# Residual turnings: one tile and one trip through DRAM for both token halves, reads issued by Pool's queue, users six steps on

## The chip, the cores and the metric

The kernel runs on one core of one Trainium2 chip. The engines that matter here are TensorE (PE in the rows; PEld is its weight load), VectorE (DVE), ScalarE (ACT), GpSimd (Pool, POOL) and SyncE (SP), each with an instruction queue of its own that runs in order. SP does no arithmetic: it issues DMA transfers, which 16 DMA engines carry out. The metric is the device time of one launch in microseconds, as a median of runs, lower being better.

## The reference

One decoder block in float32: 256 tokens, model width 2048, SwiGLU width 5632. Every matrix product keeps float32 accuracy.

```python
h = h + 0.5 * swiglu(rms_norm(h, ffn1_norm), ffn1_w_gate, ffn1_w_up, ffn1_w_down)
n = rms_norm(h, mix_norm)
rq, rk, rv, rg, sq, sk, sv = split(n @ w_in)
ret = groupnorm(retention(rope(rq), rope(rk), rv)) * silu(rg)       # 8 heads of 128, chunks of 128
swa = sliding_window_attention(rope(sq), rope(sk), sv, sinks)       # 16 query heads of 64, window 128
h = h + concat(ret, swa) @ w_out
h = h + cross_attention(rms_norm(h, xa_norm), rms_norm(mem, mem_norm))   # 4 heads of 512, 256 memory tokens
h = h + 0.5 * swiglu(rms_norm(h, ffn2_norm), ffn2_w_gate, ffn2_w_up, ffn2_w_down)
out = rms_norm(h, final_norm)
```

## The kernel before

**Products.** A float32 product is made of three: both operands are split into a rounded part and the rest (`halves`, lines 73 to 76: ScalarE writes the rounded copy, VectorE subtracts), and `three` (line 468) multiplies high by high, high by low and low by high. The weights come from DRAM in pieces of 1 MB, two steps to a piece, into three buffers `wf`, and are split into `wh` and `wl`, four buffers each.

**Steps.** `run_stream` (line 232) walks 772 steps. A step is 12 matmuls of 128 x 512 on one split weight piece: two inner blocks, two token halves of 128, three products. A clock counts the steps. In step *at* the work that has come due runs first (`run_due`), then weights are split up to three steps ahead (`prepare`, LOOKAHEAD) and fetched up to seven steps ahead (`fetch`, AHEAD), then come the matmuls. `later(d, f)` puts a piece of work d steps on. A `Unit` is one block of 512 output columns with its accumulator in PSUM; when its last step is done it calls `done`. The order of the SP queue is pinned to that of the program, so SP issues weight loads and everything else strictly one after another.

**Turnings.** The residual stream `hT` and the operands of the next product are wanted with channels on the partitions, while a unit's result has tokens there. `cross` (line 434) turns 256 tokens by 512 columns without TensorE: VectorE transposes 32 x 32 blocks of each token half (line 444), one step later SP writes each half, 256 KB, to a `box` in DRAM (line 449), two steps later SP reads each box back in four pieces of 64 KB, in which the 32-row blocks change places (line 456), and `delay` steps later (TURN, 5) the user `then` runs. There are 54 turnings: 22 in the two SwiGLUs (`up_done`, users `halves_of`), 16 at the ends of `to_h` (first down projection twice, `w_out`, `xa_wo`; the user adds to `hT`), 4 for retention's queries and keys (`rqk_done`, user `finish`), 8 for cross attention's keys and queries (`put_done`), and 4 that turn the finished residual back for the last stage (`turn_h`, user a ScalarE copy at line 948). Those four are put 6, 10, 14 and 18 steps after the second norm's last block (line 1005), at the start of the second SwiGLU.

**Work tiles.** Tiles `t2k` of 128 x 512 have ten buffers; a turning takes two, and two more for what it reads unless its caller hands in a place. `spread` (line 412) makes a row of the mix norm's factors with two transposes on TensorE; `ret_scores` (line 740) makes the retention scores two and three steps after `finish`, and `rv_done` uses them four and five steps after its own unit.

Of the kernel before, what the change touches and what calls it, by code (L numbers as in the profile page):

```python
# [17 lines left out]
P = 128  # L18
# [15 lines left out]
FIRST = 16  # L34
TURN = 5
SWA_EVERY = 5
# [3 lines left out]
def decoder_block(ctx: ExitStack, tc: tile.TileContext, a: dict, out: bass.AP):  # L40
# [20 lines left out]
    def t2k(dt=F32):  # L61
        return work.tile([P, 512], dt, tag="t2k", name=nm("t2k"), bufs=10)

# [26 lines left out]
    nc.vector.tensor_copy(identr, ident)  # L90
    ones = const.tile([P, P], F32, tag="ones", name="ones")
    nc.vector.memset(ones, 1.0)
# [265 lines left out]
    class Norm:  # L358
# [39 lines left out]
        def finish(self):  # L398

            x = self.sums  # L400
            nc.vector.tensor_tensor(x[:, :S], x[:, :S], x[:, S:], ALU.add)
            tp = tmp_ps()
            for t in range(2):
                nc.tensor.matmul(tp[:, t : t + 1], x[:, t * P : (t + 1) * P], ones[:, :1], start=True, stop=True)
            ms = sm(2, "ms")
            nc.vector.tensor_scalar(ms, tp[:, :2], 1.0 / D, EPS, ALU.mult, ALU.add)
            nc.gpsimd.tensor_tensor(self.rs, ms, mhalf[:, :2], ALU.pow)
            self.ready = True
            if self.spreads:
                later(3, self.spread)  # L410

        def spread(self):

            tp = tmp_ps()
            for t in range(2):
                rep = t2k()[:, :P]
                nc.vector.tensor_scalar(rep, ones, self.rs[:, t : t + 1], None, ALU.mult)
                nc.tensor.transpose(tp[:, t * P : (t + 1) * P], rep, ident)
            self.rows = work.tile([P, S], F32, tag="rows", name=nm("rows"), bufs=1)
            copy(self.rows, tp[:, :S])  # L420

# [11 lines left out]

    def cross(src, then, room=None, delay=TURN):

        room = [None, None] if room is None else room
        boxes = []  # L440
        out = []
        sq = [t2k() for _ in src]
        for x, v in zip(sq, src):
            nc.vector.transpose(x.rearrange("p (g q j) -> p q g j", g=4, q=4), squares_of(v))  # L444

        def write():
            for x in sq:
                boxes.append(dram.tile([P, 512], F32, tag="box", name=nm("box")))
                nc.sync.dma_start(boxes[-1], x)

        def read():
            for box, dst in zip(boxes, room):
                dst = t2k() if dst is None else dst
                far = box.rearrange("(i r) (g n) -> g r i n", i=4, g=4)
                for g in range(4):
                    nc.sync.dma_start(dst[32 * g : 32 * g + 32, :].rearrange("p (i n) -> p i n", i=4), far[g])
                out.append(dst.rearrange("p (i q j) -> p q i j", i=4, q=4))
        later(1, write)
        later(2, read)
        later(delay, lambda: then(out))  # L460

# [13 lines left out]
    def to_h(w, lhs, factor, blocks, norm=None, then=None):  # L475

        def done(acc, b):
# [11 lines left out]
            else:  # L489
                s = [t2k() for _ in range(2)]  # L490
                for t in range(2):
                    copy(s[t], acc[:, t, :], scale=factor)
                cross(s, add, s)
        for b in range(4):
            Unit(w, b, 512, lhs, lambda acc, b=b: done(acc, b), blocks, pair=True)

    def ffn(norm, w_gate, w_up, down):
# [12 lines left out]
        def up_done(b):  # L510
            def done(acc):
# [4 lines left out]
                def made(out):  # L516
                    acts[b] = halves_of(out, blk())
                cross(s, made, s)
            return done
# [193 lines left out]
    def rqk_done(g, which):  # L713
        def done(acc):
            def finish(out):
# [18 lines left out]
                if which == 1:  # L734
                    for i in range(4):
                        later(2 + i // 2, lambda i=i: ret_scores(g, i, qk))
            cross([acc[:, t, :] for t in range(2)], finish)
# [107 lines left out]
    def put_done(norm, dst, i, then=None):  # L845

        def done(acc):
            s = [scaled(acc, t, 512, norm) for t in range(2)]

            def made(out):  # L850
                dst[i] = halves_of(out, blk())
                if then is not None:
                    later(1, then)
            cross(s, made, s)
        return done
# [146 lines left out]
    def begin_ffn2(b):  # L1002
        if b == 3:
            for b in range(4):
                later(6 + 4 * b, lambda b=b: turn_h(b))

# [85 lines left out]
```

## Time and profile before

| | before |
|---|---|
| median of 3 runs | 2200.8 us |
| lowest and highest run | 2198.17 and 2201.48 us |
| profiled execution, own time | 2198.31 us |
| its span | 2196.5 us |
| TensorE busy | 2175.0 us, 99% |
| VectorE, ScalarE, GpSimd busy | 1291.7, 1027.5 and 10.4 us |
| mean granted TensorE clock | 0.998 |
| DMA | 472.04 MB, 215 GB/s |

The page gives busy time by engine, the span in 40 slices, the chain of work that ended last and the costliest lines. A busy share averages over stages, so the places where TensorE waits were looked for in the waits and in stretches of the timeline. Window rows give, for each stretch, its length and then busy time and instructions of PE, PEld, DVE, ACT and POOL, the granted clock (1.00 is 2.4 GHz, and half of that is the other level), the DMA engines' busy share and GB/s.

### The profile page before, as it was taken

Reading aid. Unit: us, or ns where it says so; the run is one execution under the profiler, and the core shown is the slowest. Engines: PE = TensorE matmul, PEld = TensorE weight load, DVE = VectorE, ACT = ScalarE, POOL = GpSimd, SP = SyncE. Lnnn points to the kernel's source line nnn. Section 1 sums busy time; section 2 is a strip of 40 time slices with the busy share of each in tenths; the row PEclk is TensorE's granted clock in tenths of the full one; section 3 lists DMA queues with packets and bytes.
Section 4 is the critical chain, followed back from the end, with each engine's and each line's share of the span. In section 5 each row is a group of like instructions: output and inputs, shape, how many; then the busy total and the mean of one; then the engine's idle time right before and its main releaser. Section 6 shows DMA issues by size and latency. Waiting matters only on the chain.

```text
span 2196.5 us, 25627 instructions
## 1 busy us (share of the span) xinstructions
PE 2175.0 (99%) x9844; PEld 1804.2 (82%) x9844; DVE 1291.7 (59%) x1536; ACT 1027.5 (47%) x1258; POOL 10.4 (0%) x17
## 2 busy tenths in 40 slices
PE   9999999999999999999999999999899999999998
PEld 7888888888888888888888888887788888888886
DVE  6555555455556778886775555575555544555554
ACT  6444444444445554544564544454444433444443
POOL 0000000000000000000000000000000000000000
PEclk9999999999999999999999999999999999999999
DMA  7766677667667555556867654676766655666663
GB/s 269 233 217 211 216 228 232 215 214 234 206 222 262 201 185 191 174 191 207 270 232 245 215 174 171 210 250 214 246 214 215 226 196 195 215 207 220 216 215 144
DMA packets 187451, 472.04 MB, mean 215 GB/s; under 512 B 15552, under 2 KB 71616, under 8 KB 187200
## 3 DMA queue, kind: packets, MB, share of 16 engines
q1 hardware_dynamic: 187040, 470.22, 63.7%
q8 instruction: 77, 1.26, 0.2%
q14 instruction: 46, 0.38, 0.1%
q10 hardware_dynamic: 288, 0.18, 0.0%
HBM read 439.93 MB, written 30.41 MB: 214 GB/s over the span
## 4 chain that ended last, share of the span: by engine, by line
PE 95%; DVE 2%; DMA 1%; issue 1%; ACT 0%; SPq 0%; ACTq 0%; POOLq 0%; POOL 0%; DVEq 0%
PE acc L471 31%; PE acc L472 31%; PE acc L470 31%; DMA wf<-in_ffn_w_up 1%; DVE wl L76 1%; PE tmp L471 0%; PE tmp L472 0%; PE tmp L470 0%; ACT wh L71 0%; PE tmp L646 0%; DMA t2k<-box 0%; PE tmp L620 0%; DVE t2k L730 0%; DVE t2k L444 0%; PE tmp L742 0%
## 5 line engine op out<-in xcount | busy, mean ns | idle before, releaser
L76 DVE TENSOR_TENSOR wl<-wf,wh 128x1024 fp32r<-128x1024 f32 (+1 forms) x776 | 942.8, 1217 | 810.0 <-ACT wh L71 803.0
L71 ACT ACTIVATE wh<-wf 128x1024 fp32r<-128x1024 f32 (+1 forms) x776 | 817.4, 1056 | 1014.1 <-PE acc L472 955.9
L470 PE MATMUL acc<-wh,blk 128*128 128x512 f32 (+1 forms) x3104 | 1208.1, 389 | 4.4 <-ACT wh L71 3.2
L471 PE MATMUL acc<-wl,blk 128*128 128x512 f32 (+1 forms) x3104 | 1206.4, 389 | 4.7 <-DVE wl L76 4.6
L472 PE MATMUL acc<-wh,blk 128*128 128x512 f32 (+1 forms) x3104 | 1205.9, 388 | 0.0
L471 PEld LDWEIGHTS acc<-wl,blk 128*128 128x128 f32 x3104 | 583.3, 188 | 125.4 <-DVE wl L76 6.8
L470 PEld LDWEIGHTS acc<-wh,blk 128*128 128x128 f32 x3104 | 583.3, 188 | 124.4 <-ACT wh L71 3.6
L472 PEld LDWEIGHTS acc<-wh,blk 128*128 128x128 f32 x3104 | 583.1, 188 | 120.7 <-DVE blk L356 0.4
L444 DVE STREAM_TRANSPOSE t2k<-t2k 128x512 f32<-128x512 f32 x76 | 49.4, 687 | 16.8 <-ACT t2k L71 16.8
L71 ACT ACTIVATE blk<-t2k 128x512 fp32r<-128x512 f32 (+2 forms) x74 | 44.8, 608 | 9.2 <-DMA t2k<-box 7.3
L76 DVE TENSOR_TENSOR blk<-t2k,blk 128x512 fp32r<-128x512 f32 (+1 forms) x66 | 44.2, 672 | 0.0
L507 ACT ACTIVATE t2k<-acc,n 128x512 f32<-128x512 f32 x44 | 27.9, 686 | 31.6 <-PE acc L472 31.5
L514 DVE SCALAR_TENSOR_TENSOR t2k<-acc,n,t2k 128x512 f32<-128x512 f32 x44 | 31.0, 746 | 15.6 <-PE acc L472 15.6
L71 ACT ACTIVATE blk<-tmp 128x512 fp32r<-128x512 f32 (+2 forms) x53 | 23.9, 459 | 27.5 <-DVE blk L76 19.0
L71 ACT ACTIVATE blk<-h,gains 128x256 fp32r<-128x256 f32 x64 | 27.3, 496 | 5.7 <-DVE h L481 5.7
L356 DVE SCALAR_TENSOR_TENSOR blk<-h,gains,blk 128x256 fp32r<-128x256 f32 x64 | 26.9, 479 | 1.7 <-ACT blk L71 1.7
L393 DVE TENSOR_TENSOR t2k<-t2k,t2k 128x512 f32<-128x512 f32 x35 | 24.0, 685 | 2.3 <-ACT t2k L389 1.0
L76 DVE TENSOR_TENSOR blk<-tmp,blk 64x256 fp32r<-64x256 f32 (+2 forms) x45 | 22.2, 494 | 4.8 <-ACT blk L71 4.5
L471 PE MATMUL tmp<-blk,blk 128*128 128x256 f32 (+1 forms) x80 | 22.6, 282 | 0.6 <-DVE blk L76 0.6
L472 PE MATMUL tmp<-blk,blk 128*128 128x256 f32 (+1 forms) x80 | 22.5, 282 | 0.0
L470 PE MATMUL tmp<-blk,blk 128*128 128x256 f32 (+1 forms) x80 | 22.5, 281 | 0.0
L481 DVE TENSOR_TENSOR h<-h,t2k 128x512 f32<-128x512 f32 x32 | 21.0, 684 | 0.0
(122 smaller groups left out, 433.0 us busy)
## 6 DMA issues: line engine op xcount, KB each, us to landing
wf<-in_ffn_w_down SPq DMA_DIRECT2D x88, 1024.0 KB, 4.9
wf<-in_ffn_w_gate SPq DMA_DIRECT2D x87, 1024.0 KB, 5.1
wf<-in_ffn_w_up SPq DMA_DIRECT2D x87, 1024.0 KB, 5.2
box<-t2k SPq DMA_DIRECT2D x108, 256.0 KB, 2.1
t2k<-box SPq DMA_DIRECT2D x432, 64.0 KB, 4.7
wf<-in_w_in_rqk SPq DMA_DIRECT2D x16, 1024.0 KB, 5.1
wf<-in_w_in_rvg SPq DMA_DIRECT2D x16, 1024.0 KB, 5.0
wf<-in_w_out SPq DMA_DIRECT2D x16, 1024.0 KB, 5.1
```

What stands on the lines that cost most here:

```text
L71: return nc.scalar.activation(dst, src, AF.Copy, **kw)
L76: nc.vector.tensor_tensor(lo, src, hi, ALU.subtract)
L356: nc.vector.scalar_tensor_tensor(x[:, k, 1, :], v[:, k, :], g, x[:, k, 0, :], ALU.mult, ALU.subtract)
L393: nc.vector.tensor_tensor(self.sums, self.sums, y, ALU.add)
L444: nc.vector.transpose(x.rearrange("p (g q j) -> p q g j", g=4, q=4), squares_of(v))
L470: nc.tensor.matmul(o, ah, bh, start=start, stop=False)
L471: nc.tensor.matmul(o, ah, bl, start=False, stop=False)
L472: nc.tensor.matmul(o, al, bh, start=False, stop=stop)
L481: nc.vector.tensor_tensor(v, v, out[t], ALU.add)
L507: nc.scalar.activation(gated[b][t], acc[:, t, :], AF.Silu, scale=norm.scale(t))
L514: nc.vector.scalar_tensor_tensor(s[t], acc[:, t, :], norm.scale(t), s[t], ALU.mult, ALU.mult)
```

## The change

`cross` takes one new tile `t4k` of 128 x 2 x 512 (two buffers) for both token halves. The two VectorE transposes write into it; SP writes it to one box of 512 KB with one DMA; four DMAs of 128 KB, now issued from Pool's queue, read it back into the same tile; the user runs six steps on instead of five. No caller hands in a place any more. `t2k` goes from ten buffers to seven, and `ones` shrinks to one column. `spread` leaves its two transposes to a piece of work two steps later. Retention's scores come four and five steps after `finish` instead of two and three. The four turnings of the residual at the second SwiGLU stand 19, 35, 51 and 67 steps on instead of 6, 10, 14 and 18.

```diff
@@ -32,7 +32,7 @@
 TAIL = 4
 WARM = 9
 FIRST = 16
-TURN = 5
+TURN = 6
 SWA_EVERY = 5
 
 
@@ -59,7 +59,7 @@
         return work.tile([P, 4, 2, S], dt, tag="blk", name=nm("blk"), bufs=13)
 
     def t2k(dt=F32):
-        return work.tile([P, 512], dt, tag="t2k", name=nm("t2k"), bufs=10)
+        return work.tile([P, 512], dt, tag="t2k", name=nm("t2k"), bufs=7)
 
     def tmp_ps(dt=F32):
         return ps_tmp.tile([P, 512], dt, tag="tmp", name=nm("tmp"))
@@ -88,7 +88,7 @@
     make_identity(nc, ident)
     nc.vector.memset(mhalf, -0.5)
     nc.vector.tensor_copy(identr, ident)
-    ones = const.tile([P, P], F32, tag="ones", name="ones")
+    ones = const.tile([P, 1], F32, tag="ones", name="ones")
     nc.vector.memset(ones, 1.0)
     warm = tmp_ps()
     for _ in range(WARM):
@@ -401,7 +401,7 @@
             nc.vector.tensor_tensor(x[:, :S], x[:, :S], x[:, S:], ALU.add)
             tp = tmp_ps()
             for t in range(2):
-                nc.tensor.matmul(tp[:, t : t + 1], x[:, t * P : (t + 1) * P], ones[:, :1], start=True, stop=True)
+                nc.tensor.matmul(tp[:, t : t + 1], x[:, t * P : (t + 1) * P], ones, start=True, stop=True)
             ms = sm(2, "ms")
             nc.vector.tensor_scalar(ms, tp[:, :2], 1.0 / D, EPS, ALU.mult, ALU.add)
             nc.gpsimd.tensor_tensor(self.rs, ms, mhalf[:, :2], ALU.pow)
@@ -411,13 +411,18 @@
 
         def spread(self):
 
-            tp = tmp_ps()
+            rep = t2k()[:, :S]
             for t in range(2):
-                rep = t2k()[:, :P]
-                nc.vector.tensor_scalar(rep, ones, self.rs[:, t : t + 1], None, ALU.mult)
-                nc.tensor.transpose(tp[:, t * P : (t + 1) * P], rep, ident)
-            self.rows = work.tile([P, S], F32, tag="rows", name=nm("rows"), bufs=1)
-            copy(self.rows, tp[:, :S])
+                nc.vector.tensor_scalar(rep[:, t * P : (t + 1) * P], ones.broadcast_to([P, P]), self.rs[:, t : t + 1], None, ALU.mult)
+
+            def turned():
+                tp = tmp_ps()
+                for t in range(2):
+                    ts = slice(t * P, (t + 1) * P)
+                    nc.tensor.transpose(tp[:, ts], rep[:, ts], ident)
+                self.rows = work.tile([P, S], F32, tag="rows", name=nm("rows"), bufs=1)
+                copy(self.rows, tp[:, :S])
+            later(2, turned)
 
         def scale(self, t):
             return self.rs[:, t : t + 1]
@@ -431,33 +436,26 @@
     def squares_of(x):
         return x if len(x.shape) == 4 else x.rearrange("p (q g j) -> p q g j", q=4, g=4)
 
-    def cross(src, then, room=None, delay=TURN):
-
-
-
-
-        room = [None, None] if room is None else room
-        boxes = []
-        out = []
-        sq = [t2k() for _ in src]
-        for x, v in zip(sq, src):
-            nc.vector.transpose(x.rearrange("p (g q j) -> p q g j", g=4, q=4), squares_of(v))
+    def cross(src, then, delay=TURN):
+
+
+
+
+        z = work.tile([P, 2, 512], F32, tag="t4k", name=nm("t4k"), bufs=2)
+        for t, v in enumerate(src):
+            nc.vector.transpose(z[:, t, :].rearrange("p (g q j) -> p q g j", g=4, q=4), squares_of(v))
+        box = dram.tile([2 * P, 512], F32, tag="box", name=nm("box"))
 
         def write():
-            for x in sq:
-                boxes.append(dram.tile([P, 512], F32, tag="box", name=nm("box")))
-                nc.sync.dma_start(boxes[-1], x)
+            nc.sync.dma_start(box.rearrange("(t p) n -> p t n", t=2), z)
 
         def read():
-            for box, dst in zip(boxes, room):
-                dst = t2k() if dst is None else dst
-                far = box.rearrange("(i r) (g n) -> g r i n", i=4, g=4)
-                for g in range(4):
-                    nc.sync.dma_start(dst[32 * g : 32 * g + 32, :].rearrange("p (i n) -> p i n", i=4), far[g])
-                out.append(dst.rearrange("p (i q j) -> p q i j", i=4, q=4))
+            far = box.rearrange("(i r) (g n) -> g r i n", r=32, g=4)
+            for g in range(4):
+                nc.gpsimd.dma_start(z[32 * g : 32 * g + 32].rearrange("p t (i n) -> p (t i) n", i=4), far[g])
         later(1, write)
         later(2, read)
-        later(delay, lambda: then(out))
+        later(delay, lambda: then([z[:, t, :].rearrange("p (i q j) -> p q i j", i=4, q=4) for t in range(2)]))
 
     def halves_of(out, x):
         for t in range(2):
@@ -490,7 +488,7 @@
                 s = [t2k() for _ in range(2)]
                 for t in range(2):
                     copy(s[t], acc[:, t, :], scale=factor)
-                cross(s, add, s)
+                cross(s, add)
         for b in range(4):
             Unit(w, b, 512, lhs, lambda acc, b=b: done(acc, b), blocks, pair=True)
 
@@ -515,7 +513,7 @@
 
                 def made(out):
                     acts[b] = halves_of(out, blk())
-                cross(s, made, s)
+                cross(s, made)
             return done
 
         for g, fbs in enumerate((range(0, 6), range(6, 11))):
@@ -733,7 +731,7 @@
                     nc.vector.tensor_tensor(dst, x, r, ALU.add)
                 if which == 1:
                     for i in range(4):
-                        later(2 + i // 2, lambda i=i: ret_scores(g, i, qk))
+                        later(4 + i // 2, lambda i=i: ret_scores(g, i, qk))
             cross([acc[:, t, :] for t in range(2)], finish)
         return done
 
@@ -851,7 +849,7 @@
                 dst[i] = halves_of(out, blk())
                 if then is not None:
                     later(1, then)
-            cross(s, made, s)
+            cross(s, made)
         return done
 
     def v_done(i):
@@ -1002,7 +1000,7 @@
     def begin_ffn2(b):
         if b == 3:
             for b in range(4):
-                later(6 + 4 * b, lambda b=b: turn_h(b))
+                later(19 + 16 * b, lambda b=b: turn_h(b))
 
     ffn(n2, a["ffn2_w_gate"], a["ffn2_w_up"], ffn2_down)
     run_stream()
```

**SP at the start of the second SwiGLU.** Before, from one weight load to the third turning of the residual (`wf` a weight buffer, `box` the DRAM tile, `t2k` the work tile; rows are queue order):

```order
L203 DMA wf_11562<-in_ffn_w_gate 128x2x1024
L449 DMA box_11576<-t2k_11554 128x512
L449 DMA box_11578<-t2k_11555 128x512
L456 DMA t2k_11596<-box_11576 32x4x128 x4
L456 DMA t2k_11601<-box_11578 32x4x128 x4
L203 DMA wf_11610<-in_ffn_w_gate 128x2x1024
L203 DMA wf_11652<-in_ffn_w_gate 128x2x1024
L449 DMA box_11672<-t2k_11644 128x512
L449 DMA box_11674<-t2k_11645 128x512
L456 DMA t2k_11695<-box_11672 32x4x128 x4
L456 DMA t2k_11700<-box_11674 32x4x128 x4
L449 DMA box_11705<-t2k_11668 128x512
```

The changed kernel, same place, from the load before the first turning of the residual:

```order
L203 DMA wf_11528<-in_ffn_w_gate 128x2x1024
L450 DMA box_11523<-t4k_11520 128x2x512
L203 DMA wf_11567<-in_ffn_w_gate 128x2x1024
L203 DMA wf_11601<-in_ffn_w_gate 128x2x1024
L203 DMA wf_11637<-in_ffn_w_gate 128x2x1024
L450 DMA box_11656<-t4k_11653 128x2x512
L203 DMA wf_11679<-in_ffn_w_up 128x2x1024
L203 DMA wf_11717<-in_ffn_w_up 128x2x1024
L203 DMA wf_11751<-in_ffn_w_up 128x2x1024
L203 DMA wf_11790<-in_ffn_w_up 128x2x1024
L203 DMA wf_11833<-in_ffn_w_gate 128x2x1024
L450 DMA box_11828<-t4k_11825 128x2x512
```

Before, 20 DMAs of turnings stand among 3 weight loads; now each single write has three or four loads between it and the next, and no read stands in SP's queue. The reads stand in Pool's queue, here those of the last `xa_wo` turning, the norm's power, and the turnings that follow:

```order
L455 DMA t4k_11033<-box_11036 32x8x128 x4
L407 TENSOR_TENSOR n_109<-ms_11235,mhalf 128x2
L455 DMA t4k_11346<-box_11349 32x8x128 x4
L455 DMA t4k_11520<-box_11523 32x8x128 x4
L455 DMA t4k_11653<-box_11656 32x8x128 x4
L455 DMA t4k_11825<-box_11828 32x8x128 x4
L455 DMA t4k_11958<-box_11961 32x8x128 x4
```

Every read of 128 KB stands in Pool's queue as one of four; the queue held 5 powers of norms, 4 of retention and 2 of the last norm before, and they keep their places between the reads.

**VectorE where retention's first queries are turned.** Before, from the scaling of the rotary table (line 429) over `finish` (lines 729 to 733):

```order
L429 TENSOR_TENSOR ctab<-ctab,rows_5543 128x512
L76 TENSOR_TENSOR wl_6227<-wf_6114,wh_6226 128x1024
L729 TENSOR_TENSOR t2k_6173<-t2k_6084,ctab 64x512
L730 TENSOR_TENSOR t2k_6173<-t2k_6084,ctab 64x512
L729 TENSOR_TENSOR t2k_6178<-t2k_6089,ctab 64x512
L731 TENSOR_TENSOR t2k_6084<-t2k_6084,ctab 128x4x4x32
L730 TENSOR_TENSOR t2k_6178<-t2k_6089,ctab 64x512
L733 TENSOR_TENSOR blk_6172<-t2k_6084,t2k_6173 128x4x128
L731 TENSOR_TENSOR t2k_6089<-t2k_6089,ctab 128x4x4x32
L444 STREAM_TRANSPOSE t2k_6244<-acc_6049 128x4x4x32
L733 TENSOR_TENSOR blk_6172<-t2k_6089,t2k_6178 128x4x128
L76 TENSOR_TENSOR blk_6040<-tmp_6183,blk_6040 128x256
```

The changed kernel, same place, lines 434 and 727 to 731, the part between two weight splits (`wl`):

```order
L631 TENSOR_TENSOR es_6015<-sinks,m_6012 128x4
L728 TENSOR_TENSOR t2k_6057<-t4k_5874,ctab 64x512
L727 TENSOR_TENSOR t2k_6062<-t4k_5874,ctab 64x512
L729 TENSOR_TENSOR t4k_5874<-t4k_5874,ctab 128x4x4x32
L635 TENSOR_TENSOR den_6014<-den_6014,es_6015 128x4
L728 TENSOR_TENSOR t2k_6062<-t4k_5874,ctab 64x512
L636 RECIPROCAL den_6014<-den_6014 128x4
L731 TENSOR_TENSOR blk_6056<-t4k_5874,t2k_6057 128x4x128
L637 TENSOR_TENSOR t2k_6001<-t2k_6001,den_6014 128x512
L76 TENSOR_TENSOR blk_5906<-tmp_6028,blk_5906 128x256
L729 TENSOR_TENSOR t4k_5874<-t4k_5874,ctab 128x4x4x32
L76 TENSOR_TENSOR wl_6068<-wf_5933,wh_6067 128x1024
```

`finish` now stands ahead of the weight split `wl_6068`, in among the softmax of a window group; before, a weight split stood between the table and `finish`, and the transposes of the next turning among its last rows.

## Rows read from the trace of the kernel before

**Rows 1.** The page's first part: busy us, share of the span, instructions.

```profile
PE 2175.0 (99%) x9844; PEld 1804.2 (82%) x9844; DVE 1291.7 (59%) x1536; ACT 1027.5 (47%) x1258; POOL 10.4 (0%) x17
```

**Rows 2.** Waits of PE, 1480 to 1580 us: total us, times, longest.

```profile
PE acc L471 <- DVE wl L76: 4.3, 2, 3.6
PE acc L470 <- ACT wh L71: 3.2, 1, 3.2
```

**Rows 3.** Windows of the second SwiGLU's start, and of the stretch behind.

```profile
1510.00:1560.00 50.00, 42.44 (x177) 33.73 (x176) 23.29 (x25) 20.38 (x25) 0.00 (x0) 0.97 0.70 224
1540.00:1550.00 10.00, 9.55 (x35) 7.73 (x36) 3.90 (x4) 3.36 (x5) 0.00 (x0) 0.83 0.63 216
1560.00:1615.00 55.00, 55.00 (x245) 45.53 (x244) 29.01 (x28) 24.55 (x26) 0.00 (x0) 1.00 0.73 248
```

**Rows 4.** Timeline of SP's queue there: start us, us, operation, count.

```profile
1501.75 1.25 SPq L449 DMA_DIRECT2D box<-t2k  x2
1510.92 3.64 SPq L456 DMA_DIRECT2D t2k<-box  x8
...
1515.60 0.40 SPq L203 DMA_DIRECT2D wf<-in_ffn_w_up  x1
...
1521.98 0.40 SPq L203 DMA_DIRECT2D wf<-in_ffn_w_up  x1
...
1532.79 0.91 SPq L203 DMA_DIRECT2D wf<-in_ffn_w_up  x2
...
1546.05 12.27 SPq L203 DMA_DIRECT2D wf<-in_ffn_w_gate  x4
```

**Rows 5.** Waits of SP's queue, 1480 to 1580 us.

```profile
SPq L456 <- DMA box<-t2k: 30.2, 6, 7.8
```

**Rows 6.** DMA issues, 1501 to 1530 us: count, KB each, us to landing.

```profile
box<-t2k SPq DMA_DIRECT2D x6, 256.0 KB, 6.3
```

**Rows 7.** DMA issues of the whole span.

```profile
box<-t2k SPq DMA_DIRECT2D x108, 256.0 KB, 2.1
```

**Rows 8.** One undisturbed turning, timelines of DVE, SP and ACT.

```profile
1601.78 1.29 DVE L444 STREAM_TRANSPOSE t2k<-t2k 128x512 f32<-128x512 f32 x2
...
1602.51 0.94 SPq L449 DMA_DIRECT2D box<-t2k  x2
...
1612.30 0.61 ACT L71 ACTIVATE blk<-t2k 128x512 fp32r<-128x512 f32 x1
1614.06 1.06 ACT L71 ACTIVATE wh<-wf 128x1024 fp32r<-128x1024 f32 x1 [1.14 <-PE acc L472]
...
1616.78 1.06 ACT L71 ACTIVATE wh<-wf 128x1024 fp32r<-128x1024 f32 x1 [1.14 <-PE acc L472]
```

**Rows 9.** Line 456, every read of a turning: minimum, median, maximum.

```profile
L456 SPq DMA_DIRECT2D t2k<-box x432: 302/430/1472, 59.1 to 2088.0; - x144
DMA to landing us min/median/max: 1.8/4.7/8.2
```

**Rows 10.** Line 407, the largest Pool work beside the start: ns minimum, median, maximum.

```profile
L407 POOL TENSOR_TENSOR nxa<-ms,mhalf x1: 869/869/869, 1111.9 to 1111.9; 128x2 f32<-128x2 f32 x1
```

**Rows 11.** The page's fifth part: VectorE's subtraction at two lengths.

```profile
L76 DVE TENSOR_TENSOR wl<-wf,wh 128x1024 fp32r<-128x1024 f32 (+1 forms) x776 | 942.8, 1217 | 810.0 <-ACT wh L71 803.0
L76 DVE TENSOR_TENSOR blk<-t2k,blk 128x512 fp32r<-128x512 f32 (+1 forms) x66 | 44.2, 672 | 0.0
```

**Rows 12.** Waits of PE, 700 to 1020 us, the three at scores and factors.

```profile
PE tmp L742 <- DVE blk L76: 0.7, 1, 0.7
PE tmp L742 <- DVE blk L733: 0.7, 1, 0.7
PE tmp L418 <- DVE t2k L417: 0.5, 1, 0.5
```

**Rows 13.** Timeline of the tail, SP's queue and DVE.

```profile
2185.59 7.24 SPq L1000 DMA_DIRECT2D out<-t2k  x8
...
2190.52 0.49 DVE L997 TENSOR_SCALAR t2k<-blk,frs 128x512 f32<-128x512 f32 x1 [0.67 <-POOL frs L990]
```

## The prediction

> **What bounds the kernel now.** I read the page's first part first. TensorE is busy for 2175.0 of the span's 2196.5 us [rows 1], so all that any reordering can win is 21.5 us, and the change removes no matrix work: the three products of every step stay as they are. The next question is where the 21.5 us lie. The waits of PE, asked in stretches, give 7.5 us at the start of the second SwiGLU (4.3 for the low parts of weights, 3.2 for the high ones [rows 2]) and 1.9 us where retention's scores and the mix norm's row of factors are made [rows 12]. Nearly all the rest stands at the first load and the last output, which the change doesn't touch.
>
> Waits don't tell the whole cost of a stall, so I counted matmuls. From 1510 to 1560 us PE ran 177; from 1560 to 1615, with no idle time, 245 [rows 3]. At the second rate 50 us would hold 245 / 55 x 50 = 222.7, so 45.7 are missing, and at 55 / 245 = 0.2245 us each the stretch **lost 10.3 us**: 7.5 us of waiting and nearly 3 us of slower running. In the worst slice, 1540 to 1550, the granted clock was 0.83 against 1.00 behind [rows 3]: part of it ran at the 1.2 GHz level, after PE had waited.
>
> Why do the weights come late there? In the timeline of SP's queue the reads of one turning's boxes stand in front of weight loads. From the writes at 1501.75 to the group of loads at 1546.05, 44.3 us, only four weight loads are issued: 1515.60, 1521.98 and two at 1532.79 [rows 4]. ScalarE's weight copies follow each other every 1616.78 - 1614.06 = 2.72 us in the steady state [rows 8]; that is one step, a load serves two steps, so 44.3 us use up 44.3 / 5.44 = 8.1 loads. The queue ahead (AHEAD, LOOKAHEAD) covers some seven steps, or 3.5 loads; the remainder is the hole. SP stood 30.2 us in six waits for boxes to land, the longest 7.8 [rows 5], because here a 256 KB box takes 6.3 us to land [rows 6] against 2.1 as the median of the span [rows 7].
>
> **The turnings at the second SwiGLU.** After the change a turning leaves one write in SP's queue and no read, and three or four weight loads stand between two of the four turnings' writes. A write's data were transposed a step earlier, so SP has nothing long to wait for. The wait that holds the loads is gone from this queue, and I take the whole loss: **-10.3 us**. What is late next? A box may still land slowly, but then Pool waits for it, and behind Pool's reads stand only powers of norms. The spacing alone would help too: the four turnings now take 48 steps, 131 us, instead of 12, 33 us.
>
> **The reads on Pool's queue.** They do not occur in the trace of before: Pool has 17 instructions in all [rows 1]. So I bound them. First, what may they cost? In an undisturbed turning the transposes stand at 1601.78 and the writes' issue ends at 1602.51 + 0.94 = 1603.45 [rows 8]; with 2.1 us to land [rows 7] the reads can start at 1605.5. The first user on ScalarE started at 1612.30, at five steps [rows 8]; at six steps it comes 2.72 us later, at 1615.0. That leaves 9.5 us without any wait. If the user waits longer, it blocks ScalarE's weight copies, which run three steps ahead: 3 x 2.72 = 8.2, less 1.06 for one copy [rows 8] and 1.22 for one subtraction [rows 11], is 5.9 us before PE notices. The room is 15.4 us for four reads, 3.9 each; with a box that lands in 6.3 us [rows 6] it is 11.2.
>
> From below: issued like SP's, at 0.302 us each, and landing 1.8 us later [rows 9], the four take 3.0 us. From above: strictly one after another, each at the longest landing seen, 8.2 us [rows 9], they take 32.8 us, 17.4 beyond the room, and over 54 turnings 940 us. I take four issues at 0.869 us, the longest single instruction on Pool in the body of the kernel [rows 10], and one median landing of 4.7 [rows 9]: 8.2 us. This is nearest to the row because SP's eight reads of a turning already share a landing of that size. It is inside both rooms: **0 us**, covered by the six steps. No gain is possible here beyond the stalls: reads that come earlier than their users serve nobody.
>
> A further count for SP: 432 reads at 0.430 us [rows 9] and half the writes leave its queue, about 190 us of issue time over the span; away from the start of the second SwiGLU nobody waited for it, so I give it nothing. The powers that now queue behind reads, at most four, wait at most one turning's reads; the norms they serve are one step later and stand three to six steps ahead of their use, 8.2 us or more.
>
> **Page against row.** VectorE's subtraction takes 1217 ns for 1024 elements and 672 ns for 512 [rows 11], 545 ns / 512 = 1.06 ns per further element: one rate. The Trainium skill, "SBUF — State Buffer", section "SBUF: two separate sides", says that a DMA issued from GpSimd has its descriptors written by GpSimd's own cores, which VectorE locks out while it runs in a two-port mode, and advises SP's or ScalarE's queue instead; by that rule the change would pay while VectorE works in such a mode. The Trainium skill, "VectorE: DVE Perf Modes", section "Why `tensor_tensor` can't do 2×_2P or 4×", says that an operation on two tensors needs the second port for its second tensor and so can't be in that mode; the one rate agrees, and by both rules most of VectorE's time would cost nothing. No run here shows the lock itself.
>
> **Retention and the last rows.** The scores come two steps later, which lets the rotated queries be ready: the two waits of 0.7 go; the factors' transposes come two steps later than VectorE's scaling, which takes 0.5: **-1.9 us** [rows 12]. But `finish` now stands ahead of a weight split among the rows of a softmax. In the four steps around it VectorE gets ten products and sums near 0.67 us, two transposes and two splits of 1.22, some 11 us against 10.9 of matmuls; the room is about what attention's own matmuls add. The price lies between 0 and 5 us, one blocked step and its repeat; I take 0, since the weight splits have three steps of lead. At the end, seven `t2k` buffers mean that the second half's first output waits for the first half's to land: issued from 2185.59, needed at 2190.52 [rows 13], 4.9 us against a landing below 4.7 by the nearest row [rows 9]. That is 0 again, and some 3 us if one lands at 8.2.
>
> **The sum.** 2198.3 (own time of the profiled execution) - 10.3 - 1.9 = 2186.1. The median of the runs is 2200.8, 2.5 above that execution; carried over, **2188.6 us**, or about 2188.5.
>
> **The rivals.** A: *the transfers don't queue, they share.* If the loads were late because all transfers together were too many, then another issuing queue wins nothing and only the scores' gain stays: 2198.9. Against it: the DMA engines were busy at 0.70 in the stalled stretch and at 0.73 in the one behind, which lost nothing [rows 3]; and SP is seen waiting [rows 5]. The Trainium skill, "DMA: Bandwidth & Descriptors", section "Issuing engines are not separate DMA queues", speaks for A: a second issuer saves only the time of issuing, usually small beside the transfer. Here the row differs from it, since SP's 30.2 us of waits are the time at stake and not the issue itself.
>
> B: *half the gain.* The box lands late, the reads follow late, and some of the four turnings' users block ScalarE; half of 10.3 comes back: 2193.7.
>
> D: *VectorE is late at retention.* The price of 5 us falls due, for one or for two groups of heads, and A's or B's loss may add to it: 2193.5 to 2203.
>
> C, **slower**: *Pool's reads go one after another.* If Pool finishes with each read before the next, at the median landing of 4.7, they take 18.8 us [rows 9], 3.4 beyond the room; ScalarE then blocks in each of 54 turnings, and the cost is 184 us: about 2370. The point from which it decides is 15.4 us for four reads, 3.9 each. For it: no row shows Pool issuing anything. A version of it is VectorE keeping Pool from working: busy 59% of the span [rows 1], it would stretch 8.2 us to 8.2 / 0.41 = 20 us, 4.6 beyond the room, some 250 us in all. The Trainium skill's page "SBUF — State Buffer", as told above, names this mechanism. Against it: the subtraction's single rate, and that reads on a queue have so far been seen to overlap.
>
> **How the numbers follow.** The forecast, with 2185 to 2194 as its own range, has 0.70; B 0.08; A 0.07; D 0.08; C 0.07. A measurement of this kernel can tell about 0.2%, 4.4 us, from no change, so faster means below 2196.4 and slower above 2205.2. Faster: forecast, B and a fifth of D, 0.80. Slower: C and a few outcomes of D, 0.09. Within: 0.11. The range takes in the forecast, B, A and most of D: 2184 to 2202; C is left out, since it is far away and has less than one in ten.
>
> **What would show it.** In the changed kernel's waits of PE around 1480 to 1580 us the weights' rows should be gone; every 55 us there should hold about 245 matmuls at clock 1.00; SP should have no wait for a box. Pool's four reads should end within 9.5 us of the box's landing, and ScalarE's splits of turned tiles should not wait for them. The score waits should be gone and no weight wait take their place around `finish`. I am wrong if ScalarE or VectorE is seen waiting for turned tiles throughout (C), or if weights are late at the second SwiGLU with SP idle (A).

## The result: 2185.4 us, and the profile after

| | before | after |
|---|---|---|
| median | 2201.0 us | 2185.4 us |
| lowest and highest run | 2198.2 and 2201.5 us | 2184.7 and 2186.2 us |
| profiled execution, own time and span | 2198.3 and 2196.5 us | 2186.15 and 2184.4 us |

Both medians are of four runs; the 2200.8 us ahead of the prediction was of three. The changed kernel is faster: ratio 0.9932, 95% interval 0.9915 to 0.9949. The prediction was 2188.5 us, 2184 to 2202.

The page's first part, to be set against [rows 1]:

```profile
PE 2171.3 (99%) x9844; PEld 1803.3 (83%) x9844; DVE 1290.9 (59%) x1536; ACT 1028.1 (47%) x1258; POOL 135.4 (6%) x233
```

TensorE runs the same 9844 matmuls in 3.7 us less of busy time, and its idle time falls from 21.5 to 13.1 us: 12.1 us of span together. The first fits matmuls that ran at the lower clock level before (granted clock 0.83 in the worst slice of [rows 3]). All waits of PE in the changed kernel, over the whole span (total us, times, longest):

```profile
PE acc L468 <- ACT blk L71: 2.3, 2, 1.7
PE tmp L95 <- POOL ident masks.py:199: 1.4, 1, 1.4
PE tmp L404 <- DVE t2k L401: 0.5, 1, 0.5
PE acc L469 <- DVE wl L76: 0.4, 2, 0.2
```

The 7.5 us for weights [rows 2] and the waits at scores and factors [rows 12] are gone. Two stretches of windows, first of the kernel before, then of the changed one:

```profile
1495.00:1550.00 55.00, 51.02 (x216) 41.17 (x215) 26.52 (x28) 25.64 (x31) 0.00 (x0) 0.97 0.70 221
1550.00:1605.00 55.00, 51.42 (x227) 42.25 (x226) 31.17 (x31) 24.25 (x25) 0.00 (x0) 1.00 0.68 242
```

```profile
1495.00:1550.00 55.00, 55.00 (x244) 45.57 (x243) 31.32 (x33) 26.78 (x29) 4.63 (x8) 1.00 0.70 230
1550.00:1605.00 55.00, 55.00 (x245) 45.53 (x244) 29.84 (x29) 24.58 (x27) 6.91 (x12) 1.00 0.78 255
```

In the same 110 us the changed kernel runs 489 matmuls instead of 443: 46 x 0.2245 us = 10.3 us. From 730 to 1095 us PE was idle 2.5 us before and 0.2 after. Against that, the waits at the start are 1 us longer and a new one of 0.5 us stands at line 404. -10.3 - 2.3 + 1.0 + 0.5 = -11.1 of the span's -12.1; the rest is spread.

SP's queue there, to be set against [rows 4]:

```profile
1486.75 14.33 SPq L203 DMA_DIRECT2D wf<-in_ffn_w_gate  x3
1504.38 0.37 SPq L450 DMA_DIRECT2D box<-t4k  x1
1505.49 15.51 SPq L203 DMA_DIRECT2D wf<-in_ffn_w_up  x4
1526.58 0.37 SPq L203 DMA_DIRECT2D wf<-in_ffn_w_gate  x1
1527.79 0.37 SPq L450 DMA_DIRECT2D box<-t4k  x1
1530.87 11.24 SPq L203 DMA_DIRECT2D wf<-in_ffn_w_gate  x3
```

Eight loads are issued from 1505.49 to 1542 us, where [rows 4] had four in 44.3. Pool's reads (line 455: issue ns, then us from issue to landing) and ScalarE's wait for them (total us, times, longest):

```profile
L455 POOL DMA_DIRECT2D t4k<-box x216: 582/582/745, 62.1 to 2075.4; - x108
...
DMA to landing us min/median/max: 3.0/5.1/9.5
```

```profile
ACT blk L71 <- DMA t4k<-box: 34.0, 26, 3.9
```

### The profile page after: what moved, and what is told of

It reads as the page before. It is cut to its first block, busy times and chain, and to the rows that moved or that the text cites. A ratio compares the mean times of both kernels' runs of the same rounds, so it can differ in the third digit from the quotient of the medians.

```text
span 2184.4 us, 25213 instructions
## 1 busy us (share of the span) xinstructions
PE 2171.3 (99%) x9844; PEld 1803.3 (83%) x9844; DVE 1290.9 (59%) x1536; ACT 1028.1 (47%) x1258; POOL 135.4 (6%) x233
## 4 chain that ended last, share of the span: by engine, by line
PE 95%; DVE 2%; issue 2%; DMA 1%; ACT 0%; POOL 0%; SPq 0%; POOLq 0%; ACTq 0%; DVEq 0%
PE acc L469 31%; PE acc L468 31%; PE acc L470 31%; DVE wl L76 1%; PE tmp L470 0%; PE tmp L469 0%; PE tmp L468 0%; DMA t4k<-box 0%; DMA wf<-in_ffn_w_up 0%; PE tmp L618 0%; PE tmp L644 0%; ACT wh L71 0%; POOL t4k L455 0%; PE tmp L740 0%; DVE t4k L446 0%
## 5 line engine op out<-in xcount | busy, mean ns | idle before, releaser
L455 POOL DMA_DIRECT2D t4k<-box x216 | 124.7, 584 | 1759.9 <-DMA box<-t4k 1034.6
L446 DVE STREAM_TRANSPOSE t4k<-t2k 128x512 f32<-128x512 f32 x76 | 49.3, 687 | 13.9 <-ACT t2k L71 13.9
L71 ACT ACTIVATE blk<-t4k 128x512 fp32r<-128x512 f32 (+1 forms) x68 | 39.1, 623 | 34.0 <-DMA t4k<-box 34.0
L76 DVE TENSOR_TENSOR blk<-t4k,blk 128x512 fp32r<-128x512 f32 x60 | 38.7, 687 | 14.5 <-ACT blk L71 14.4
L479 DVE TENSOR_TENSOR h<-h,t4k 128x512 f32<-128x512 f32 x32 | 20.6, 685 | 4.1 <-DMA t4k<-box 4.1
L468 PE MATMUL tmp<-blk,blk 128*128 128x256 f32 (+1 forms) x80 | 22.6, 282 | 0.0
L469 PE MATMUL tmp<-blk,blk 128*128 128x256 f32 (+1 forms) x80 | 22.5, 282 | 0.0
```

The costliest lines, as they stand in the source:

```text
L71: return nc.scalar.activation(dst, src, AF.Copy, **kw)
L76: nc.vector.tensor_tensor(lo, src, hi, ALU.subtract)
L446: nc.vector.transpose(z[:, t, :].rearrange("p (g q j) -> p q g j", g=4, q=4), squares_of(v))
L455: nc.gpsimd.dma_start(z[32 * g : 32 * g + 32].rearrange("p t (i n) -> p (t i) n", i=4), far[g])
L468: nc.tensor.matmul(o, ah, bh, start=start, stop=False)
L469: nc.tensor.matmul(o, ah, bl, start=False, stop=False)
```

## The experiments

The diffs are against the kernel named; times are medians, and ratios are to the kernel before in the same session.

### Where the 10 us come from: spacing, queue, merging

**Spacing alone.** The kernel before with

```diff
-                later(6 + 4 * b, lambda b=b: turn_h(b))
+                later(19 + 16 * b, lambda b=b: turn_h(b))
```

> The kernel before with one thing changed: the four turnings of the residual at the second SwiGLU stand 19, 35, 51 and 67 steps on instead of 6, 10, 14 and 18. Reads stay in SP's queue, in pieces of 64 KB. Theory Q (weight loads are late because they stand behind reads that wait for their box in SP's queue, several turnings in a row): one turning at a time holds SP for a few us, which the seven steps of lead cover; the 10 us at the second SwiGLU go, the 2.5 us at retention stay: 2188 to 2191 us. Rival S (the queue itself must be freed, each turning by itself loses): 2195 us or more, with weight waits of PE spread over four places. Rival M (the merging into one tile and fewer DMAs is what counts): no change, 2199 to 2201.

2188.7 us, ratio 0.9947 (0.9930 to 0.9963). No wait for weights is left at the second SwiGLU; all waits at scores and factors are still there. The stretch that ran 216 matmuls before:

```profile
1495.00:1550.00 55.00, 55.00 (x244) 45.53 (x244) 31.23 (x32) 27.48 (x30) 0.00 (x0) 1.00 0.71 232
```

The spacing alone is enough for the 10 us; S and M as the only remedy are out.

**Pool's queue, old spacing.** The kernel before with

```diff
-TURN = 5
+TURN = 6
-                    nc.sync.dma_start(dst[32 * g : 32 * g + 32, :]...
+                    nc.gpsimd.dma_start(dst[32 * g : 32 * g + 32, :]...
```

> The kernel before with the reads issued from Pool's queue, eight of 64 KB for each turning, and users six steps on; spacing as before (6, 10, 14, 18). Theory Q: SP is free, so the weights come in time although the turnings stand close: PE's waits of 7.5 us at the second SwiGLU go, 2188 to 2191 us; eight issues of 0.58 us take 4.7 us and the reads land some 2 us later than in the changed kernel, inside ScalarE's and VectorE's lead. Rival W (the spacing is what counts): 2196 us or more, the waits for weights at 1510 to 1560 us still there.

2186.3 us, 0.9936 (0.9922 to 0.9951): the same place is free of waits without any spacing. The same stretch, and the loads issued from 1500 to 1530 us:

```profile
1495.00:1550.00 55.00, 55.00 (x245) 45.53 (x244) 33.94 (x37) 29.87 (x36) 20.33 (x39) 1.00 0.88 283
```

```profile
wf<-in_ffn_w_up SPq DMA_DIRECT2D x4, 1024.0 KB, 8.0
```

W as the only remedy is out. Pool's queue and the sixth step were changed together here, and the sixth step was not tried by itself in the kernel before, so which of the two removes the stall is open.

**Reads from SP, all else as changed.** The changed kernel with `nc.sync` for the four reads.

> The changed kernel with the four reads of a turning issued from SP's queue instead of Pool's; spacing, merging and six steps stay. Theory Q: SP waits for each box for 3 us or so, and one such wait at a time is covered by the lead: 2185 to 2189. Rival S (Pool's queue is needed): 2193 or more, with PE waiting for weights at several turnings.

2185.3 us, 0.9931 (0.9916 to 0.9946): as the changed kernel. SP's waits in this kernel, over the whole span:

```profile
SPq L455 <- DMA box<-t4k: 99.2, 50, 5.8
```

The kernel before, over the whole span, and then from 1501.75 to 1546.05 us, the stretch in which the prediction counted loads:

```profile
SPq L456 <- DMA box<-t2k: 35.9, 11, 7.8
```

```profile
SPq L456 <- DMA box<-t2k: 21.0, 4, 7.8
```

Over the whole span SP waits 99.2 us for boxes here against 35.9 before, and nothing is lost. The difference is where the waits stand: the 30.2 us of [rows 5] lie in 100 us, 21.0 of them in the 44.3 us in which too few loads went out; with the spacing, the same 100 us hold 14.8. So waiting for a box on SP's queue costs nothing by itself; the 10 us were lost where four such waits came within 45 us. Pool's queue, beside the spacing, earns nothing.

**Old spacing in the changed kernel.** With `later(6 + 4 * b, ...)`.

> The changed kernel with the old spacing of the four turnings (6, 10, 14, 18). Theory Q: reads stand in Pool's queue, so SP's loads aren't held; as the changed kernel within 2 us, 2185 to 2188. Rival W (spacing): the loss of about 10 us comes back, 2195 to 2198.

2194.0 us, 0.9964 (0.9951 to 0.9977): a loss of 8.6 us against the changed kernel in the median, 4.4 in the span of the profiled execution. My expectation failed, though reads stand in Pool's queue. DMA issues from 1500 to 1530 us (count, KB, us to landing) and then the waits of ScalarE from 1495 to 1560 and of SP from 1480 to 1580:

```profile
wf<-in_ffn_w_up SPq DMA_DIRECT2D x4, 1024.0 KB, 10.9
...
t4k<-box POOLq DMA_DIRECT2D x12, 128.0 KB, 8.0
```

```profile
ACT wh L71 <- DMA wf<-in_ffn_w_up: 13.7, 4, 5.4
...
ACT blk L71 <- DMA t4k<-box: 6.2, 1, 6.2
```

```profile
SPq L450 <- DVE t4k L446: 29.9, 6, 13.8
```

SP and ScalarE there:

```profile
1507.56 1.40 SPq L203 DMA_DIRECT2D wf<-in_ffn_w_up  x2
```

```profile
1517.92 1.06 ACT L71 ACTIVATE wh<-wf 128x1024 fp32r<-128x1024 f32 x1 [5.42 <-DMA wf<-in_ffn_w_up]
```

Weight loads now land after 10.9 us (5.4 in the changed kernel) while twelve reads run beside them from another queue, and ScalarE waits 5.42 us for one of the two issued at 1507.56. Turned tiles come late, there are only two `t4k` buffers, so the transposes of the third turning stand behind the user of an earlier one; SP's write waits 13.8 us for them, with the loads behind it. This is what the trace shows, not a cause shown: reads from Pool at the old spacing did no harm in the kernel before, where loads landed after 8.0 us, and two buffers do none in the next run.

**Both undone.** Reads from SP and `later(6 + 4 * b, ...)`; one tile, one write, four reads and six steps stay.

> The changed kernel with both steps undone: reads from SP's queue and the four turnings 6, 10, 14 and 18 steps on; one tile, one write and four reads for a turning stay, with two buffers. Theory Q: either step alone removed the stall, so with both gone it is back, SP waits for boxes for 15 us or more between 1480 and 1600 us and PE for weights: 2194 to 2200 us. Rival M (the merging alone would do): 2185 to 2188.

2185.4 us, 0.9925 (0.9910 to 0.9940): no stall. My expectation failed again; M's time is right, though the sixth step is in this run as well. SP's waits from 1480 to 1580 us, issues from 1500 to 1530, and SP's order:

```profile
SPq L455 <- DMA box<-t4k: 12.6, 4, 6.7
```

```profile
wf<-in_ffn_w_up SPq DMA_DIRECT2D x4, 1024.0 KB, 7.3
...
box<-t4k SPq DMA_DIRECT2D x4, 512.0 KB, 3.4
t4k<-box SPq DMA_DIRECT2D x12, 128.0 KB, 6.1
```

```profile
1507.63 0.42 SPq L203 DMA_DIRECT2D wf<-in_ffn_w_up  x1
1508.14 5.97 SPq L455 DMA_DIRECT2D t4k<-box  x8
1514.59 0.39 SPq L203 DMA_DIRECT2D wf<-in_ffn_w_up  x1
```

A box of double size lands in 3.4 us instead of the 6.3 of [rows 6], and SP waits 12.6 us instead of 30.2. Counted as in the prediction: from behind the load at 1500.06 to 1538.36 us this kernel issues five weight loads where 38.3 / 5.44 = 7.0 are used, 2.0 short, inside the lead of 3.5; before it was 8.1 - 4 = 4.1 short. Which of fewer DMAs, larger boxes and the sixth step (it moves the turnings of `xa_wo` against those of the residual) does it was not separated.

Against the run above, only the queue of the reads differs: at the old spacing Pool's queue costs this kernel 8.6 us. From SP the reads stand between two loads, from Pool they run beside both. The count of loads doesn't tell the two apart: from behind its load at 1499.96 to the one at 1523.28 us, the kernel that stalls issues two where 23.3 / 5.44 = 4.3 are used, 2.3 short and inside the lead too. What differs in the traces is the loads' landing, 10.9 us against 7.3.

### What the sixth step is worth

The changed kernel with `TURN = 5`, and with `TURN = 4`.

> The changed kernel with users five steps on instead of six. ScalarE waited 34 us in 26 turnings for turned tiles at six steps, 3.9 at most; at five every wait is 2.7 us longer and the turnings without a wait begin to have one: some 120 to 180 us. Theory L (the lead of 5.9 us takes such waits): only the longest, 3.9 + 2.7 = 6.6, shows, PE waits under 3 us in all, 2185 to 2189 us. Rival N (there is no such lead, six steps are needed): each us that ScalarE waits more costs one, 2250 us or more.

> The changed kernel with users four steps on. ScalarE's waits are 5.4 us longer than at six steps, 5 to 9 us each, about the lead of 5.9 us or past it. Theory L: past the lead a turning costs the difference, 0 to 3.5 us in each of 54, together 40 to 100 us: 2225 to 2290 us. Rival N: 54 x 5.4 = 290 us more, about 2470. Rival F (the lead is larger than I worked out): 2185 to 2195.

2196.2 us, 0.9975 (0.9966 to 0.9984), and 2197.7 us, 0.9988 (0.9978 to 0.9997). Both expectations failed, in size and place. The windows of the kernel before, of the changed one, then of five and of four steps, at the end of cross attention:

```profile
1440.00:1495.00 55.00, 55.00 (x245) 45.31 (x245) 37.07 (x44) 26.23 (x33) 0.70 (x1) 1.00 0.70 229
```

```profile
1440.00:1495.00 55.00, 55.00 (x246) 45.43 (x244) 34.96 (x42) 26.40 (x32) 5.32 (x9) 1.00 0.71 233
```

```profile
1440.00:1495.00 55.00, 48.64 (x202) 39.18 (x201) 30.33 (x38) 21.58 (x28) 6.24 (x9) 0.94 0.70 221
```

```profile
1440.00:1495.00 55.00, 46.70 (x195) 37.59 (x194) 29.41 (x37) 21.42 (x28) 6.22 (x9) 0.94 0.68 213
```

Nearly the whole loss is one new stall, at the last turnings of `xa_wo`: against the changed kernel 44 matmuls or 9.9 us at five steps, 51 or 11.4 at four, part of it at the 1.2 GHz level (clock 0.94) after PE had waited. Pool and VectorE there at five steps, and how long the reads issued from 1460 to 1485 us took to land, in the changed kernel and at five steps:

```profile
1468.01 2.30 POOL L455 DMA_DIRECT2D t4k<-box  x4 [20.73 <-DMA box<-t4k]
```

```profile
1479.91 1.29 DVE L479 TENSOR_TENSOR h<-h,t4k 128x512 f32<-128x512 f32 x2 [8.44 <-DMA t4k<-box]
```

```profile
t4k<-box POOLq DMA_DIRECT2D x4, 128.0 KB, 3.7
```

```profile
t4k<-box POOLq DMA_DIRECT2D x4, 128.0 KB, 8.9
```

The reads end 11.9 us after Pool began, the sum into `hT` holds VectorE for 8.44 us with weight splits behind it, and the lead of 5.9 us is not enough. That is the consequence rival C named, a user that waits past the lead, at one place; its mechanism is not seen, since Pool issues the four reads within 2.30 us and they land 8.9 us later, so they overlap. The kernel before runs users at five steps without a stall here, and so does the run with two numbers below: it is the rest of the change that makes the sixth step necessary, and which part of it was not tried. At the other turnings PE loses next to nothing: ScalarE's waits for turned tiles are 39.9 us at five steps and 31.5 at four, near the 34.0 at six, though VectorE's sums wait 20.3 and 24.2 us for them in all, against 4.1 at six. The reason is in the build: for the SwiGLU turnings ScalarE's instructions stand in the same order at four and at six steps. One of them, ScalarE at six steps, and at four (the turned tile's write was issued at 143.53 and at 142.51 us):

```profile
156.73 1.15 ACT L71 ACTIVATE blk<-t4k 128x512 fp32r<-128x512 f32 x2 [1.19 <-DMA t4k<-box]
```

```profile
156.07 1.15 ACT L71 ACTIVATE blk<-t4k 128x512 fp32r<-128x512 f32 x2 [1.54 <-DMA t4k<-box]
```

13.2 and 13.6 us after the write: the step given to `later` doesn't set when the user runs here.

### Retention, queues and issue

**Scores as before.** The changed kernel with `later(2 + i // 2, ...)`.

> The changed kernel with retention's scores two and three steps after finish, as before. My term for them is 1.4 us (two waits of 0.7 us): the waits come back and the profiled span grows by 1 to 3 us, 2186 to 2189. Rival: finish stands elsewhere among VectorE's work now, and the scores find their operands ready anyway: no wait, 2185 to 2186.

2188.0 us, 0.9937 (0.9922 to 0.9952), span 1.7 us longer. The two waits come back, in all PE's waits of that kernel:

```profile
PE tmp L740 <- DVE blk L731: 0.7, 1, 0.7
...
PE tmp L740 <- DVE den L635: 0.7, 1, 0.7
```

**Two numbers alone.** The kernel before with the spacing and `later(4 + i // 2, ...)`, and nothing else.

> The kernel before with only two numbers changed: the residual's turnings 19, 35, 51 and 67 steps on, and retention's scores four and five steps after finish. No merging, reads on SP's queue, users five steps on, ten t2k buffers. Theory Q with the small term: both gains are there, 10 us at the second SwiGLU and 1.4 us at the scores: 2186 to 2188 us, within 1 us or so of the whole change. Rival: merging and Pool's queue hold part of the gain: 2189 or more.

2185.8 us, 0.9933 (0.9917 to 0.9950): the whole gain of the change, with two tiles, SP's queue, five steps and ten buffers. The stretch of the stall:

```profile
1495.00:1550.00 55.00, 55.00 (x244) 45.57 (x243) 32.13 (x33) 26.90 (x30) 0.00 (x0) 1.00 0.71 231
```

So the merging, Pool's queue, the sixth step and the later transposes of `spread` together earn nothing that shows beside these two numbers.

**Reads from ScalarE's queue.** The changed kernel with `nc.scalar` for the reads.

> The changed kernel with the reads issued from ScalarE's queue. ScalarE's queue runs in order, so its weight copies now stand behind reads that wait for a box: 1 to 4 us in each of 54 turnings. Theory L: the lead of 5.9 us takes them: 2185 to 2190 us. Rival N: 54 x 2 us or so show, 2290.

2190.1 us, 0.9952 (0.9937 to 0.9967). L holds in the main, at the end of its range, 4.6 us above the changed kernel: ScalarE's weight copies start 60.1 us late in 21 places (11.2 in 7 in the changed kernel), 4.1 us at most, where the profile shows nothing that they wait for but their queue; little of it shows: from 730 to 1095 us, around retention, PE is idle 3.4 us instead of 0.2, with one wait of 2.5 us for a weight split.

**Eight reads from Pool.** The changed kernel, each read cut into its two token halves.

> The changed kernel with each turning's reads as eight of 64 KB from Pool's queue. Before, the same eight took 0.548 us each to issue against 0.582 for 128 KB, so the issue of a turning takes 4.4 us instead of 2.3: ScalarE's waits for turned tiles grow by up to 2 us a turning, to 80 to 150 us from 34, and the lead covers them: no change of the time, 2184 to 2187. Rival C (Pool's share is at its limit): 2200 or more.

2184.4 us in one execution, 0.3 us below the fastest of the changed kernel's four. ScalarE's waits for turned tiles double to 69.1 us in 35, less than the 80 to 150 expected, and no loss of time shows: Pool's share was not at its limit.

**VectorE beside Pool's issue.** Added to `cross` in the changed kernel:

```diff
         later(2, read)
+
+        def port():
+            for _ in range(5):
+                nc.vector.tensor_copy(ctab[:, 512:1024], ctab[:, :512])
+        if clock[0] > 560:
+            later(1, port)
+            later(2, port)
```

> The changed kernel with five copies of 128 x 512 on VectorE, from one half of the dead rotary table to the other, one and two steps after each turning of the second SwiGLU, so that some run while Pool issues the reads. The copies have one source and lie in SBUF: the kind of work which by the Trainium skill, SBUF - State Buffer, section SBUF: two separate sides, locks GpSimd out while it writes descriptors. By the page the reads' issue, 0.582 us each in 215 of 216 cases or so, becomes longer where a copy runs, by up to the copy's own 0.3 us or more. My theory, that Pool's issue doesn't depend on VectorE here: 0.582 throughout, and the time within 3 us of the changed kernel's, VectorE's extra 3.3 us a turning being idle time.

2185.3 us in one execution. The copies, two groups of Pool's reads, the first without a longer issue and the second with, and four copies beside a third group:

```profile
L461 DVE COPY ctab<-ctab 128x512 f32<-128x512 f32 x100 | 43.2, 432 | 2.1
```

```profile
1620.50 2.31 POOL L455 DMA_DIRECT2D t4k<-box  x4 [24.03 <-DVE ctab L461]
...
1680.65 2.47 POOL L455 DMA_DIRECT2D t4k<-box  x4 [14.35 <-DVE ctab L461]
```

```profile
1943.05 2.10 DVE L461 COPY ctab<-ctab 128x512 f32<-128x512 f32 x4
```

In the same stretch of the changed kernel all ten groups take 2.30 or 2.31 us; here four of ten take 2.41 to 2.47. So the copies do lengthen the issue, against my expectation of none, by 0.17 us at most. In two other groups the issue stays at 2.30 us and the four copies that start beside it take 2.10 and 2.01 us, where four in a row take 1.80 to 1.85 us elsewhere: there the delay falls on VectorE.

## Why the prediction was right, and where it was not

**The size at the second SwiGLU.** -10.3 us was forecast and 10.3 measured, and the own time of the profiled execution came to 2186.15 us against 2186.1 worked out. The count of missing matmuls, and not the 7.5 us of waits, gave the right size: the wait took the clock down too. But the size doesn't test the mechanism, since any edit that removes the stall returns it, and the agreement to 0.1 us is partly luck: retention gave 0.4 us more than worked out, the start and the wait at line 404 took 1.5, and about 1 us is spread over the span.

**The cause was half right.** That SP's in-order queue let only four loads through in 44.3 us fits the runs from SP's queue (4.1 short before, with the stall; 2.0 short with the reads in one tile, without). It gives no size: beyond the lead of 3.5 only 0.6 of a load is missing, 3.3 us, and PE waited 7.5. But I put it to the reads in that queue as such, and took the queue as the remedy and the spacing as help. The 30.2 us of waits that I called the time at stake belong to 100 us; 21.0 of them lie in the stretch that I counted. With the spacing, SP's queue carries 99 us of waits for nothing lost. Without it, Pool's queue with a sixth step is enough in the kernel before and fails in the changed one, where SP's queue does not fail. So several turnings close together stand behind each stall seen at this place, but two kernels have them and no stall; the spacing removed it wherever it was tried. Of the change as it stands, the spacing is needed, since with Pool's queue it loses 8.6 us without it; Pool's queue is not. Two numbers give the whole gain, so the prediction was right in its time with a remedy, the queue, that earns nothing.

**The queues, page and row.** I weighed a sentence of the Trainium skill, "DMA: Bandwidth & Descriptors", section "Issuing engines are not separate DMA queues", and held that the rows differ from it, because SP's waits were the time at stake. At the new spacing the runs agree with the page: 2185.3 us from SP, 2185.4 from Pool. At the old spacing, in the changed kernel, they do not: 2185.4 us from SP and 2194.0 from Pool, so there the issuing queue matters, and the second queue is the worse one.

**The room for the reads.** The measured reads take 2.3 us to issue and 5.1 to land at the median, against 8.2 taken for both; where ScalarE or VectorE was seen waiting for them, it started 7 to 11 us after Pool's first issue. The term of 0 held. But the step "at six steps it comes 2.72 us later" failed: the user's place in ScalarE's queue is the build's, and the reads outlast the time without waits by 1.3 us on average in 26 turnings, which the lead takes. Where the sixth step counts is a single place, the end of `xa_wo`, worth 10.7 us in the changed kernel, which I had not looked at: I took the undisturbed turning of [rows 8] for all 54 and didn't ask where VectorE's sum stands in front of weight splits. With five steps two thirds of the gain would be gone (2196.2 us), though the two numbers alone keep all of it at five.

**Retention and the tail.** -1.9 us forecast, -2.3 measured; VectorE's denser `finish` cost nothing that shows. The last outputs kept their pace, with VectorE waiting 0.67 us for Pool as in [rows 13]:

```profile
2178.44 0.49 DVE L995 TENSOR_SCALAR t2k<-blk,frs 128x512 f32<-128x512 f32 x1 [0.67 <-POOL frs L988]
```

**From the execution to the median.** The term of +2.5 us was wrong: the changed kernel's median is 0.7 below its profiled execution, and the error of the prediction, about 3 us, is this term alone. In one session the kernel before ran from 2197.0 to 2203.8 us in 19 executions and five steps from 2191.8 to 2199.6 in ten; every kernel without a stall that was run four times stays within 2.3 us. That fits a stall that differs from run to run, so that the offset of a kernel with one goes with the stall; only one execution of each was profiled, so this isn't shown. The profiled execution of before happened to be among its shortest.

**The rule against Pool's queue.** The Trainium skill, "SBUF — State Buffer", section "SBUF: two separate sides", told of VectorE holding up what Pool issues. The added copies (432 ns for what a subtraction takes 672 to do) show its direction, in four groups of ten, and a price of 0.17 us at most for four reads; the time of the kernel doesn't show it.

## What to carry to other kernels

Count what a queue lets through in a stretch against what is used up there, and compare with the lead; the total of the waits on the queue says little, since 99 us spread over the span cost nothing and 21 us within 44 went with a loss of 10. Look at how long the loads take to land as well: one kernel here stalled with its count inside the lead. When several edits aim at one stall, each may remove it alone: try the cheapest (here, two numbers) before merging buffers, which can make another edit necessary. An offset between a profiled run and a median should not be carried over from a kernel whose stall is to be removed.

## What the runs showed that was not expected

The issue of a read on Pool costs nearly the same for 64 KB (0.548 us) as for 128 KB (0.582 us), and it hardly varies. A box of 512 KB in one DMA landed sooner (3.4 us) than two of 256 KB (6.3 us) at the crowded place; what stood ahead of each in the queue differs too, so this isn't a price of the size. Loads that share the DMA engines with reads from another queue landed in 10.9 us, and in 7.3 with the same reads in their own queue; but in the kernel before, with as many bytes in 64 KB reads from Pool, they landed in 8.0, so this isn't a price of the queue alone.
